# SwiGLU stages of a decoder trunk: the moving operands' addresses shifted against the standing operands'

## The chip, the cores and the metric

The kernel runs on one core of one Trainium2 chip. The metric is device time in microseconds (us) of one execution; lower is better. A core has a matrix engine (PE, with its weight loads listed apart as PEld), a vector engine (DVE), a scalar engine (ACT), GpSimd (POOL) and queues that start transfers (SP among them). It works on a scratch memory of 128 partitions; every address below is a byte address within a partition, the same in all 128.

## The reference

Two layers over x (512 tokens, width 1024, float32). In each, x takes half a SwiGLU, a mixer, and half a SwiGLU again, each after an RMSNorm:

```python
def _swiglu(h, wg, wu, wd):
    return (jax.nn.silu(h @ wg) * (h @ wu)) @ wd
...
    for l in range(DEPTH):
        h = _rmsnorm(x, ffn_pre_norm[l])
        x = x + 0.5 * _swiglu(h, ffn_pre_w_gate[l], ffn_pre_w_up[l], ffn_pre_w_down[l])
        ...
        h = _rmsnorm(x, ffn_post_norm[l])
        x = x + 0.5 * _swiglu(h, ffn_post_w_gate[l], ffn_post_w_up[l], ffn_post_w_down[l])
```

So there are four SwiGLU stages, with 2816 hidden columns each. The first layer's mixer is retention beside dilated attention, the second's is gated linear attention.

## The kernel before

All matrix products are done with operands split into a high and a low half (`hi` and `lo`, each 4 bytes an element), in three matmuls that add up in one accumulator: high by high, high by low, low by high. In a plain product (`mm3`, lines 205 to 207) the *standing* operand is a 128x128 piece of a weight tile (`whi`, `wlo`) and the *moving* one 512 tokens of an activation (`xgh`, `xgl`). Before each matmul PE loads the standing operand's 128 columns; that load shows as PEld.

In a SwiGLU stage (`ffn`) the first four hidden tiles go through plain products. The other 18 are made in pairs by the seven-product form (a Strassen-like scheme: seven products of half-size blocks in place of eight). `moving` builds its moving operands once for each stage: four tiles `hh` (high) and four `hl` (low), each seven slots of 256 tokens. `block_plan` loads a 1 MB piece of weights (`raw`) and makes the standing operands from it: `whi` and `wlo` for two of the seven products, and sums and differences of blocks, `shi` (made in `high`) and `slo` (made in `low`), for the other five. `product` then runs four k-steps of three matmuls, 256 moving columns each:

```python
    mm(out, lhsT=w[0][:, s], rhs=hi, ...)   # line 404: hh moving, whi or shi standing
    mm(out, lhsT=w[0][:, s], rhs=lo, ...)   # line 405: hl moving, the same standing
    mm(out, lhsT=w[1][:, s], rhs=hi, ...)   # line 406: hh moving, wlo or slo standing
```

Down products (`down_tile`, plain, 512 columns) are put between them. At the end of the last stage `last_half` runs plain products of 256 columns, half the tokens at a time.

Tiles of a stage come from one pool, `self.fpool`. A tile name gets its place when it is first asked for, right behind the one before. In a stage the order is `head`, `part` (2), `sg` (2), `hh` (4), `hl` (4), `raw` (2), `s3`, `space`, `shi` (6), `slo` (6). `space` is asked for in `high` at the first call of a stage, is never written, and only takes up room: 16 elements, 64 bytes. The long-lived tiles (`xgh`, `xgl`, `whi`, `wlo`) lie in other pools at fixed addresses.

**Distance**, in this text, is the address of a standing operand less that of the moving operand that streams while it is being loaded, as a remainder by 512 bytes. A standing piece is 512 bytes wide, a slot of `hh` 1024 and a row of 512 tokens 2048, so all pieces of a tile have the same remainder. In the program as built the remainders by 512 are:

```
tile                                  remainder     standing tile against it    distance
xgh, xgl (moving)                     384           whi, wlo 384                0
hh, hl (moving)                       320           whi, wlo, shi, slo 384      64
cath, catl of the first mixer         320           whi, wlo 384                64
cath, catl of the second mixer        0             whi, wlo 384                384
xgh (moving), ones_r (loaded)         384           ones_r 128                  256
diag (moving), whi (loaded)           96            whi 384                     288
xgh (moving), p (loaded)              384           p 320                       448
xgh (moving), sp (loaded)             384           sp 0                        128
```

`cath` and `catl` are the mixers' concatenated outputs, moving operands of their output projections (`out_steps`, 512 columns). `ones_r`, `p` and `sp` are small standing operands of the mixers and norms; each is loaded once or a few times right behind a plain product.

Of the kernel before, what the change touches and what calls it, by code (L numbers as in the profile page):

```python
# [19 lines left out]
P = 128  # L20
# [14 lines left out]
GROUPS = ((0, 1), (2, 3), (4, 5), (6, 7), (8,), (9, 10))  # L35
BLOCKS = ((2, 3), (4, 5), (6, 7), (8, 9), (10,))
XGB = 9

RET_HEADS, RET_DK = 4, 128
DIL_HEADS, DIL_DH = 8, 64  # L40
# [10 lines left out]
class Trunk:  # L51
    def __init__(self, ctx, tc, a):
# [3 lines left out]
        self.keep = pool("keep", bufs=1)  # L56
        self.xg = pool("xg", bufs=XGB)
        self.wpool = pool("wpool", bufs=4)
# [54 lines left out]
    def block_plan(self, src):  # L113


        nc = self.nc
        st = {}
        q = [slice(i * T, (i + 1) * T) for i in range(4)]

        def high(key, x):  # L120
            if not self.spaced:
                self.spaced = True
                self.t2k(self.fpool, "space", bufs=1, shape=[P, 16])
            hi = self.t2k(self.fpool, "shi", F32R, SUMS, shape=[P, T])
            nc.scalar.copy(out=hi, in_=x)  # L125
            st[key] = (hi, x)

        def low(key):
            hi, x = st[key]
            lo = self.t2k(self.fpool, "slo", F32R, SUMS, shape=[P, T])  # L130
            nc.vector.tensor_tensor(out=lo, in0=x, in1=hi.bitcast(F32), op=ALU.subtract)  # L131
            return hi, lo

        def add(out, a, b):
            nc.vector.tensor_tensor(out=out, in0=a, in1=b, op=ALU.add)  # L135

        def c0():
            raw = st["raw"] = self.t2k(self.fpool, "raw", shape=[P, 4 * T], bufs=2)
            nc.sync.dma_start(out=raw, in_=src)
            hi = self.t2k(self.wpool, "whi", F32R, shape=[P, WC])  # L140
            lo = self.t2k(self.wpool, "wlo", F32R, shape=[P, WC])
            nc.scalar.copy(out=hi, in_=raw[:, :WC])
            st["s3"] = self.t2k(self.fpool, "s3", bufs=1)
            add(st["s3"], raw[:, q[0]], raw[:, q[2]])
            add(raw[:, q[2]], raw[:, q[2]], raw[:, q[3]])
            high("s1", raw[:, q[2]])
            nc.vector.tensor_tensor(out=lo, in0=raw[:, :WC], in1=hi.bitcast(F32), op=ALU.subtract)
            add(raw[:, q[0]], raw[:, q[0]], raw[:, q[2]])
            return hi, lo

        def s1():
            high("s2", st["raw"][:, q[0]])
            return low("s1")

        def s2():
            raw = st["raw"]
            high("s3", st["s3"])
            add(raw[:, q[1]], raw[:, q[1]], raw[:, q[0]])
            return low("s2")

        def s3():
            high("a22", st["raw"][:, q[3]])
            return low("s3")

        def a22():
            high("s4", st["raw"][:, q[1]])
            return low("a22")

        def s4():
            return low("s4")  # L170

        return [("w", c0), ("s", s1), ("s", s2), ("s", s3), ("s", a22), ("s", s4)]
# [269 lines left out]
    def ffn(self, f, nxt):  # L442
        nc, tc = self.nc, self.tc
        gi = (0, 2, 3, 5)[f]
        with tc.tile_pool(name=self.uid("ffn"), bufs=1, reuse_waits="tile") as self.fpool, self.banks(pj=7, sc=1):
            self.act, self.hs, self.spaced = [], [], False
            new_sg = lambda: self.t2k(self.fpool, "sg", bufs=2, shape=[P, 2 * T])

            def glu(g, u, out):
                us = self.t2k(self.fpool, "part", bufs=2, shape=[P, 3 * H])[:, :T]  # L450
                nc.vector.tensor_tensor(out=out, in0=g, in1=self.rrow, op=ALU.mult)
                nc.scalar.activation(out=out, in_=out, func=AF.Silu)
                nc.vector.tensor_tensor(out=us, in0=u, in1=self.rrow, op=ALU.mult)
                nc.vector.tensor_tensor(out=out, in0=us, in1=out, op=ALU.mult)


            held, heads = [], []
            build = self.moving(gi)

            def head():  # L460
                n, g, u = held.pop(0)
                if n % 2 == 0:
                    heads.append(self.t2k(self.fpool, "head", shape=[P, 2 * T], bufs=1) if n == 0 else new_sg())
                glu(g, u, heads[-1][:, n % 2 * T:(n % 2 + 1) * T])

            for n in range(2 * HEAD):
                held.append((n, self.proj_t(), self.proj_t()))
                if n > 0:
                    head()
                    next(build, None)  # L470
                    next(build, None)
            head()
            for sg in heads:
                self.keep_act(sg)

            for before, group in zip(GROUPS, BLOCKS):
                calls = 4 * len(group)
                order = [KD * (i + 1) // calls - KD * i // calls for i in range(calls)]
                tiles = iter(range(KD))
                share = iter(order)  # L480

                def fill():
                    for _ in range(next(share)):
                        self.down_tile(next(tiles), before, False, nxt)

                for p in group:
                    sg = new_sg()
                    a, c = self.block(fill)
                    nc.scalar.activation(out=sg[:, :T], in_=c[:, :T], func=AF.Silu)
                    nc.scalar.activation(out=sg[:, T:T + H], in_=a[:, :H], func=AF.Silu, scale=-1.0)  # L490
                    nc.scalar.activation(out=sg[:, T + H:], in_=c[:, T:], func=AF.Silu, scale=-1.0)
                    a, c = self.block(fill)
                    neg = dict(scalar=-1.0, op0=ALU.mult, op1=ALU.mult)
                    nc.vector.tensor_tensor(out=sg[:, :T], in0=c[:, :T], in1=sg[:, :T], op=ALU.mult)
                    nc.vector.scalar_tensor_tensor(out=sg[:, T:T + H], in0=a[:, :H], in1=sg[:, T:T + H], **neg)
                    nc.vector.scalar_tensor_tensor(out=sg[:, T + H:], in0=c[:, T:], in1=sg[:, T + H:], **neg)
                    self.keep_act(sg)
            self.last_group(GROUPS[-1], nxt)
# [22 lines left out]
    def last_group(self, group, nxt):  # L521
# [5 lines left out]
        for d in range(KD):  # L527
# [14 lines left out]
            for e, w, at, ps in first:  # L542
# [4 lines left out]
                nc.vector.scalar_tensor_tensor(out=self.x[e], in0=ps, scalar=0.5, in1=self.x[e], op0=ALU.mult, op1=ALU.add)  # L547
                if nxt is not None and e < XGB - n:
                    self.scaled(e, nxt)
                self.squares(e)  # L550
            first = []
        if nxt is not None:
            for e in range(XGB - n, KD):
                self.scaled(e, nxt)
# [561 lines left out]
```

## Time and profile before

| what | value |
|---|---|
| median of 3 runs | 1919.24 us (1919.2 to 1923.63) |
| the profiled execution | 1920.47 us, span 1918.7 us |
| PE busy | 1889.4 us, 98% of the span |
| DVE, ACT busy | 1383.0 us (72%), 850.2 us (44%) |
| mean granted clock of TensorE | 0.993 of full speed |

Busy time of PE says little by itself: matmuls overlap in the profile (one of 256 columns is listed with 281 ns, and the next starts long before its end). What counts is the time from one matmul's start to the next one's start, called a **pass** below. Lines of the timeline give start and duration in us; L404 is line 404 of the kernel before, and an arrow reads output from inputs.

### The profile page before, as it was taken

Reading aid. Unit: us, or ns where it says so; the run is one execution under the profiler, and the core shown is the slowest. Engines: PE = TensorE matmul, PEld = TensorE weight load, DVE = VectorE, ACT = ScalarE, POOL = GpSimd, SP = SyncE. Lnnn points to the kernel's source line nnn. Section 1 sums busy time; section 2 is a strip of 40 time slices with the busy share of each in tenths; the row PEclk is TensorE's granted clock in tenths of the full one; section 3 lists DMA queues with packets and bytes.
Section 4 is the critical chain, followed back from the end, with each engine's and each line's share of the span. In section 5 each row is a group of like instructions: output and inputs, shape, how many; then the busy total and the mean of one; then the engine's idle time right before and its main releaser. Section 6 shows DMA issues by size and latency. Waiting matters only on the chain.

```text
span 1918.7 us, 28135 instructions
## 1 busy us (share of the span) xinstructions
PE 1889.4 (98%) x11360; PEld 1660.4 (87%) x11360; DVE 1383.0 (72%) x2114; ACT 850.2 (44%) x1377; POOL 90.1 (5%) x69
## 2 busy tenths in 40 slices
PE   8999999999999999999999999999999999999996
PEld 6899999877777889999988999998788888999995
DVE  7987786744555897777679878776466579777864
ACT  5544444433332554444445444444434245544441
POOL 1000000200000200000020000002000020000001
PEclk9999999999999999999999999999999999999998
DMA  5222222321111423332132322222222142323211
GB/s 199 99 104 106 100 100 78 123 77 66 50 66 39 165 88 112 109 104 105 67 124 92 110 103 100 99 89 85 88 77 67 56 156 89 118 100 110 100 67 44
DMA packets 43061, 183.81 MB, mean 96 GB/s; under 512 B 4897, under 2 KB 7201, under 8 KB 33714
## 3 DMA queue, kind: packets, MB, share of 16 engines
q1 hardware_dynamic: 39888, 177.75, 26.6%
q10 hardware_dynamic: 3042, 4.26, 0.7%
q8 instruction: 89, 1.46, 0.3%
q14 instruction: 42, 0.34, 0.1%
HBM read 179.89 MB, written 2.10 MB: 95 GB/s over the span
## 4 chain that ended last, share of the span: by engine, by line
PE 95%; DVE 3%; issue 1%; ACT 0%; POOL 0%; DMA 0%; POOLq 0%; DVEq 0%; SPq 0%; ACTq 0%
PE pj L205 17%; PE pj L206 17%; PE pj L207 17%; PE pj L404 12%; PE pj L406 12%; PE pj L405 12%; PE sc L740 1%; PE o L768 1%; PE sc L280 1%; PE sc L298 0%; PE sc L815 0%; PE tp L756 0%; DVE xgl L253 0%; DVE wlo L107 0%; PE o L972 0%
## 5 line engine op out<-in xcount | busy, mean ns | idle before, releaser
L205 PE MATMUL pj<-xgh,whi 128*128 128x512 f32 x1260 | 506.2, 402 | 8.0 <-ACT whi L106 7.1
L206 PE MATMUL pj<-xgl,whi 128*128 128x512 f32 x1260 | 493.2, 391 | 1.1 <-DVE xgl L253 1.0
L207 PE MATMUL pj<-xgh,wlo 128*128 128x512 f32 x1260 | 492.6, 391 | 0.0
L405 PE MATMUL pj<-hl,shi 128*128 128x256 f32 x1440 | 404.9, 281 | 1.5 <-DVE hl L394 1.5
L404 PE MATMUL pj<-hh,shi 128*128 128x256 f32 x1440 | 405.0, 281 | 0.8 <-ACT hh L392 0.8
L406 PE MATMUL pj<-hh,slo 128*128 128x256 f32 x1440 | 404.7, 281 | 0.0
L106 ACT CAST whi<-wraw 128x1024 fp32r<-128x1024 f32 x189 | 197.8, 1047 | 254.2 <-PE pj L206 164.1
L125 ACT CAST shi<-raw 128x512 fp32r<-128x512 f32 x288 | 178.5, 620 | 288.1 <-PE pj L405 232.6
L205 PEld LDWEIGHTS pj<-xgh,whi 128*128 128x128 f32 x1260 | 238.2, 189 | 62.0 <-issue 12.1
L107 DVE TENSOR_TENSOR wlo<-wraw,whi 128x1024 fp32r<-128x1024 f32 x189 | 236.1, 1250 | 65.5 <-ACT whi L106 64.9
L207 PEld LDWEIGHTS pj<-xgh,wlo 128*128 128x128 f32 x1260 | 237.9, 189 | 50.3 <-DVE wlo L107 0.8
L406 PEld LDWEIGHTS pj<-hh,slo 128*128 128x128 f32 x1440 | 276.6, 192 | 0.1
L206 PEld LDWEIGHTS pj<-xgl,whi 128*128 128x128 f32 x1260 | 238.2, 189 | 43.2 <-DVE xgl L253 2.2
L405 PEld LDWEIGHTS pj<-hl,shi 128*128 128x128 f32 x1440 | 270.5, 188 | 4.6 <-DVE hl L394 1.7
L404 PEld LDWEIGHTS pj<-hh,shi 128*128 128x128 f32 x1440 | 270.5, 188 | 4.0 <-ACT hh L392 1.1
L131 DVE TENSOR_TENSOR slo<-raw,shi 128x512 fp32r<-128x512 f32 x288 | 197.1, 687 | 83.4 <-ACT shi L125 83.3
L405 PE MATMUL pj<-hl,whi 128*128 128x256 f32 x576 | 162.3, 282 | 0.5 <-DVE hl L393 0.5
L404 PE MATMUL pj<-hh,whi 128*128 128x256 f32 x576 | 162.3, 282 | 0.1
L406 PE MATMUL pj<-hh,wlo 128*128 128x256 f32 x576 | 162.0, 281 | 0.0
L135 DVE TENSOR_TENSOR raw<-raw 128x512 f32<-128x512 f32 x216 | 148.5, 688 | 3.0
L519 DVE SCALAR_TENSOR_TENSOR x<-pj,x 128x512 f32<-128x512 f32 x160 | 109.6, 685 | 50.7 <-PE pj L207 50.7
L270 POOL TENSOR_TENSOR sqa<-sqa,sq 128x512 f32<-128x512 f32 x41 | 64.0, 1561 | 1061.8 <-issue 645.2
(201 smaller groups left out, 2375.0 us busy)
## 6 DMA issues: line engine op xcount, KB each, us to landing
raw<-in_w_blk SPq DMA_DIRECT2D x72, 1024.0 KB, 4.8
wraw<-in_w_down SPq DMA_DIRECT2D x88, 512.0 KB, 3.2
wraw<-in_w_gu SPq DMA_DIRECT2D x32, 512.0 KB, 3.2
wraw<-in_w_dqk SPq DMA_DIRECT2D x8, 512.0 KB, 3.4
wraw<-in_w_rqk SPq DMA_DIRECT2D x8, 512.0 KB, 3.3
wraw<-in_w_eo SPq DMA_DIRECT2D x8, 512.0 KB, 3.2
wraw<-in_w_gr SPq DMA_DIRECT2D x8, 512.0 KB, 3.3
wraw<-in_w_gv SPq DMA_DIRECT2D x8, 512.0 KB, 3.2
```

The costliest lines, as they stand in the source:

```text
L106: self.halved = nc.scalar.copy(out=hi[:, :cols], in_=raw[:, :cols]).ins
L107: nc.vector.tensor_tensor(out=lo[:, :cols], in0=raw[:, :cols], in1=hi[:, :cols].bitcast(F32), op=ALU.subtract)
L125: nc.scalar.copy(out=hi, in_=x)
L131: nc.vector.tensor_tensor(out=lo, in0=x, in1=hi.bitcast(F32), op=ALU.subtract)
L135: nc.vector.tensor_tensor(out=out, in0=a, in1=b, op=ALU.add)
L205: mm(out, lhsT=w[0], rhs=x[0], start=first, stop=False)
L206: mm(out, lhsT=w[0], rhs=x[1], start=False, stop=False)
L207: self.last = mm(out, lhsT=w[1], rhs=x[0], start=False, stop=last).ins
L404: mm(out, lhsT=w[0][:, s], rhs=hi, start=first and k == 0, stop=False, skip_group_check=True)
L405: mm(out, lhsT=w[0][:, s], rhs=lo, start=False, stop=False, skip_group_check=True)
L406: self.last = mm(out, lhsT=w[1][:, s], rhs=hi, start=False, stop=k == KD // 2 - 1, skip_group_check=True).ins
L519: nc.vector.scalar_tensor_tensor(out=self.x[d], in0=ps, scalar=0.5, in1=self.x[d], op0=ALU.mult, op1=ALU.add)
```

## The change

Each stage gets a number of its own from `SHIFTS`. A tile `shift` of that many elements, never written, is asked for first in the stage's pool, so all tiles up to `s3` lie that much higher. `space` grows to 144 elements less the shift, so `shi` and `slo` lie 512 bytes higher in all four stages and keep their remainder.

```diff
+SHIFTS = (32, 48, 64, 80)
...
         def high(key, x):
             if not self.spaced:
                 self.spaced = True
-                self.t2k(self.fpool, "space", bufs=1, shape=[P, 16])
+                self.t2k(self.fpool, "space", bufs=1, shape=[P, 144 - self.shift])
...
             self.act, self.hs, self.spaced = [], [], False
+            self.shift = SHIFTS[f]
+            self.t2k(self.fpool, "shift", bufs=1, shape=[P, self.shift])
```

From the two programs as built, the remainders of `hh` and `hl` and their distance to the standing operands:

```
stage (f)   shift, bytes   hh, hl before   hh, hl after   distance before   distance after   after, by 256
1 (0)       128            320             448            64                448              192
2 (1)       192            320             0              64                384              128
3 (2)       256            320             64             64                320              64
4 (3)       320            320             128            64                256              0
```

No instruction is added, removed or moved: on all five engines the two programs list the same instructions in the same order. The waits are the same too, but for two transfers at the head of stage 3 (line 139, `raw`): the first `raw` now waits for two earlier transfers where it waited for one, and the second for none where it waited for one, because the shifted buffer overlaps both `raw` buffers of stage 2.

## Rows read from the trace of the kernel before

**Rows 1.** The page, busy time by engine and the chain that ended last.

```profile
PE 1889.4 (98%) x11360; PEld 1660.4 (87%) x11360; DVE 1383.0 (72%) x2114; ACT 850.2 (44%) x1377; POOL 90.1 (5%) x69
...
PE 95%; DVE 3%; issue 1%; ACT 0%; POOL 0%; DMA 0%; POOLq 0%; DVEq 0%; SPq 0%; ACTq 0%
```

**Rows 2.** Windows of stages 1 and 4, line 404 alone: window, length, PE busy, PEld.

```profile
55.28:336.50 281.22, 142.32 (x504) 94.80 (x503) 0.99 0.28 100
...
1600.51:1873.79 273.28, 141.62 (x504) 94.42 (x503) 1.00 0.28 99
```

**Rows 3.** Timeline, seven-product form: start us, duration us, engine, line.

```profile
318.34 0.28 PE L404 MATMUL pj<-hh,shi 128*128 128x256 f32 x1
318.34 0.19 PEld L405 LDWEIGHTS pj<-hl,shi 128*128 128x128 f32 x1
...
320.46 0.28 PE L404 MATMUL pj<-hh,shi 128*128 128x256 f32 x1
```

**Rows 4.** Timeline, plain products of 256 columns at the end of stage 4.

```profile
1895.67 0.28 PE L206 MATMUL pj<-xgl,whi 128*128 128x256 f32 x1
...
1897.47 0.28 PE L206 MATMUL pj<-xgl,whi 128*128 128x256 f32 x1
```

**Rows 5.** Timeline, plain products of 512 columns, xgh and xgl moving.

```profile
1888.07 0.39 PE L205 MATMUL pj<-xgh,whi 128*128 128x512 f32 x1
...
1891.47 0.39 PE L205 MATMUL pj<-xgh,whi 128*128 128x512 f32 x1
```

**Rows 6.** Timeline, first mixer's output projection, cath and catl moving.

```profile
609.83 0.39 PE L206 MATMUL pj<-catl,whi 128*128 128x512 f32 x1
...
612.16 0.39 PE L207 MATMUL pj<-cath,wlo 128*128 128x512 f32 x1
```

**Rows 7.** Timeline, second mixer's output projection, cath and catl moving.

```profile
1529.71 0.40 PE L207 MATMUL pj<-cath,wlo 128*128 128x512 f32 x1
...
1532.04 0.40 PE L207 MATMUL sc<-cath,wlo 128*128 128x512 f32 x1
```

**Rows 8.** Timeline, a plain product followed by a matmul on ones_r.

```profile
1346.25 0.39 PE L207 MATMUL pj<-xgh,wlo 128*128 128x512 f32 x1
1346.25 0.19 PEld L298 LDWEIGHTS sc<-diag,ones_r 128*128 128x128 f32 x1
...
1346.47 0.40 PE L298 MATMUL sc<-diag,ones_r 128*128 128x512 f32 x1
1346.71 0.40 PE L205 MATMUL pj<-xgh,whi 128*128 128x512 f32 x1
```

**Rows 9.** Timeline, a plain product followed by transposes of p.

```profile
444.94 0.40 PE L207 MATMUL pj<-xgh,wlo 128*128 128x512 f32 x1
444.95 0.48 PEld L756 LDWEIGHTS tp<-ident,p 128*128 128x128 f32 x3
...
445.18 0.38 PE L756 MATMUL tp<-ident,p 128*128 128x128 f32 x2
```

**Rows 10.** Timeline, a plain product followed by matmuls on sp.

```profile
1453.94 0.40 PE L207 MATMUL pj<-xgh,wlo 128*128 128x512 f32 x1
1453.95 0.54 PEld L965 LDWEIGHTS o<-e,sp 128*128 128x128 f32 x3
...
1454.18 0.38 PE L965 MATMUL o<-e,sp 128*128 128x128 f32 x2
```

**Rows 11.** Timeline, short matmuls of the second mixer, 128 moving columns each.

```profile
1442.16 1.06 PE L939 MATMUL sc<-e,e 128*128 128x128 f32 x8
1443.05 1.06 PE L877 MATMUL sc<-cum,la 128*128 128x128 f32 x8
```

**Rows 12.** Head of stage 3: last reads of raw, its first transfer, first use.

```profile
L131 DVE TENSOR_TENSOR slo<-raw,shi x3: 685/693/693, 939.4 to 947.9; 128x512 fp32r<-128x512 f32 x3
...
959.64 0.42 SPq L139 DMA_DIRECT2D raw<-in_w_blk  x1
...
972.78 0.68 DVE L135 TENSOR_TENSOR s<-raw 128x512 f32<-128x512 f32 x1
```

## The prediction

> **What bounds the kernel now.** I read the page first. PE is busy 98% of the span, and the chain that ended last lies on PE for 95% [rows 1]; no other engine is near. So the time changes if a matmul's pass changes, and hardly otherwise. Then the windows by stage: line 404 has 504 matmuls in each stage [rows 2], lines 405 and 406 as many, so the seven-product form has 3 x 504 = 1512 passes a stage and 6048 in all. The granted clock there is 0.99 to 1.00 [rows 2] of full speed, the level of 2.4 GHz. Then the timeline, for the pass itself. From 318.34 to 320.46 there are 18 passes in 2.12 us, 117.8 ns each [rows 3]. 6048 such passes are 712 us, 37% of the span. That is the part of the time that the change can touch.
>
> The reader should also see in [rows 3] when the next standing operand is read: the load for line 405 starts at 318.34, with the matmul of line 404. So PE reads two streams at a time, the moving one of this matmul and the standing one of the next, and the address between them is what the change alters.
>
> **Does the address matter?** The trace has other distances. With 512 columns, xgh and xgl moving against whi and wlo (distance 0) take 15 passes in 3.40 us, 226.7 ns [rows 5]. The output projections do the same work with cath and catl moving: 10 passes in 2.33 us, 233 ns, at distance 64 [rows 6], and again 2.33 us for 10 at distance 384 [rows 7]. With 256 columns, the end of stage 4 has distance 0: 15 passes in 1.80 us, 120.0 ns [rows 4], against 117.8 at distance 64 in the seven-product form [rows 3]. So it matters by 2 to 6 ns, and not in the same direction: 0 is the cheaper of the two at 512 columns and the dearer at 256. With 256 columns the moving stream is so short that the load lies beside all of it; either stream can be the one that is late.
>
> A rule of the Trainium skill speaks against any effect. "TensorE: Matmul & The Clock Gate", section "Step-by-step: what each phase is for", gives PE two independent read ports and says that loading the next weights takes no bandwidth from the running matmul; "SBUF — State Buffer", section "Who interferes with whom", says that PE never waits on anyone. By that rule the sum below is 0 in every stage; the trace disagrees, with 117.8 against 120.0 ns and 226.7 against 233 ns for equal work at different addresses.
>
> **After what distance does the pattern repeat?** Single passes of 512 columns help. While ones_r is loaded the distance is 256: that pass goes from 1346.25 to 1346.47, 0.22 us, and the next, diag against whi at distance 288, takes 0.24 [rows 8]. There are eleven passes like the first (32.79 to 1566.98 us); ten last 226 to 228 ns, as at distance 0, and one 230. At distance 448 (p) the pass is 0.24 us [rows 9] and at 128 (sp) also 0.24 [rows 10]; the others on p and sp right behind xgh take 230 to 238 ns. So at 512 columns 256 acts like 0, and 128, 448, 64, 384 and 288 all act unlike it. I take it that the pattern repeats every 256 bytes. Starts are rounded to 10 ns in these rows and each is a single pass, so this is likely, not sure.
>
> **The change, part by part.** The two tiles that only take up room cost no instruction, and every engine's list is the same as before, so nothing queues differently. One wait is new: the first raw transfer of stage 3 has to find both raw buffers of stage 2 free. The last read of raw in stage 2 starts at 947.9 and takes 0.7 us, the transfer starts at 959.64, and its data is first used at 972.78 [rows 12]. It finds both free for 11 us, so this costs 0; were that cover gone, a transfer would have the 13 us to its first use before PE noticed. The plain products keep their addresses and cost 0. What is left is 1512 passes a stage, each at its new distance:
>
> Stage 3, distance 320, which is 64 by 256: the pass of now, 117.8 ns, and 0 us. If the pattern does not repeat by 256, it is as open as stages 1 and 2.
>
> Stage 4, distance 256, which is 0 by 256: the nearest rows of the same width are [rows 4], 120.0 ns. 1512 x 2.2 ns = +3.4 us.
>
> Stage 1 (448, or 192 by 256) and stage 2 (384, or 128): no pass of 256 columns at these distances is in the trace. From below: a pass can't be shorter than its load. Eight matmuls of 128 columns, which hide none of it, take 0.89 us from 1442.16 to 1443.05, 111.2 ns each [rows 11]; 117.8 less 111.2 is 6.5 ns, so at best -9.9 us a stage. From above: the largest steady difference between two distances is the 6.3 ns from [rows 5] to [rows 6], so +9.5 us a stage; the largest seen at 256 columns is 2.2 ns, +3.4 us. At 512 columns 448, 384 and 128 belong with 64, not with 0 [rows 6, 7, 9, 10], so I put both stages at the row of 64, 117.8 ns, and 0 us.
>
> The sum is 0 + 0 + 0 + 3.4 = +3.4 us. On the profiled execution, 1920.47 us (1.8 us more than its span), that makes 1923.9. The profiled execution was 1.2 us above the median of the runs, 1919.24, so the median should be 1922.6 us, 0.18% up. A measurement of this kernel can tell about 0.3% from no change, 5.8 us, which is 0.95 ns on each of the 6048 passes.
>
> **The rivals.**
>
> *64 is the one good distance at 256 columns, and the others cost what 0 costs.* For it: the only other distance seen at this width is the dearer one, and at 512 columns too there is one good class and a wide bad one. Against it: at 512 columns 128, 384 and 448 go with 64. It is decided by stages 1 and 2. If one of them takes 120.0 ns, the sum is +6.7 us, 1926.0; if both do, +10.1 us, 1929.3; with stage 3 too, +13.4 us, 1932.7. From two of the four stages on it is slower by over 0.3%.
>
> *At 128 or 192 the two streams keep clear of each other and the load alone sets the pass.* This is the other side: faster. For it: 117.8 is still 6.5 ns above what a load takes alone [rows 3, 11], so some conflict is left at distance 64, and a place half a period away may avoid it. Against it: at 512 columns no distance gets below the 226.7 ns of distance 0, and the two streams, one covering 1024 bytes while the other covers 512, must cross at some point wherever they start. One stage at 111.2 ns makes -9.9 + 3.4 = -6.5 us, 1912.7; both make -16.4 us, 1902.9. It comes out faster by over 0.3% once stages 1 and 2 together give back 9.2 us, that is 3 ns a pass.
>
> *The change does nothing:* the 2.2 ns between [rows 3] and [rows 4] come from the code around them (last_half is a short run behind a stage, with other tiles), not from the distance. Then 1919.2. Against it: the 15 passes of [rows 4] are all alike, and [rows 5] and [rows 6] do equal work. The rule of the Trainium skill named above ("TensorE: Matmul & The Clock Gate") ends here too.
>
> **How the numbers follow.** My forecast (stage 4 dearer, the rest within a few tenths of a ns) gets 0.46. No effect gets 0.08, and mixtures in which a loss and a gain nearly cancel 0.04. The first rival, in one of its forms, gets 0.29, and the second 0.13. So within 0.3%: 0.46 + 0.08 + 0.04 = 0.58; slower 0.29; faster 0.13. The range reaches down to one stage at the load's floor, 1912.7, rounded to 1912, and up to both stages 1 and 2 at 120.0 ns, 1929.3, rounded to 1930. It leaves out about 0.07 below (both stages at the floor) and 0.11 above (stage 3 too, or passes over 120 ns).
>
> **What the profile after would show.** Stage by stage, count the passes in a stretch like [rows 3]: I expect 117.8 ns in stages 1, 2 and 3 and 120.0 in stage 4, and stage 4's window longer by 3.4 us with the others unchanged. Stage 3 away from 117.8 says that the pattern doesn't repeat by 256. Stage 4 at 117.8 says that [rows 4] were about something else. Stage 1 or 2 at 111 is the second rival, and at 120 or above the first. The plain products should stay at 226.7 ns, and PE should not wait for raw at the head of stage 3. The prediction is wrong if the four stages' mean pass moves by more than 0.95 ns; the least supported step is that 128 and 192 do what 64 does.

## The result and the profile after

The changed kernel takes 1930.72 us in the median (1928.43 to 1933.4, 4 runs) beside 1919.22 us (1918.98 to 1923.63, 4 runs) for the kernel before on the same chip. The ratio is 1.0055, with a 95% interval of 1.0034 to 1.0076: 0.55% slower, by more than the 0.3% named above. The forecast was 1922.6 us and no change that can be told; the median is 0.7 us above the top of the range.

From the page of the changed kernel, busy time by engine and the chain that ended last, to be put beside [rows 1]:

```profile
PE 1902.5 (98%) x11360; PEld 1668.7 (86%) x11360; DVE 1383.9 (72%) x2114; ACT 851.1 (44%) x1377; POOL 90.1 (5%) x69
...
PE 95%; DVE 3%; issue 1%; ACT 0%; POOL 0%; DMA 0%; POOLq 0%; DVEq 0%; SPq 0%; ACTq 0%
```

As many instructions as before on every engine, and the chain still lies on PE: what moved is the time of PE's own passes. The windows of the four stages, line 405 alone (the line that was 404), set from a stage's first seven-product matmul to its last, to be put beside [rows 2] (window, length, PE busy, PEld busy, granted clock, DMA share, GB/s):

```profile
54.93:337.25 282.32, 141.77 (x504) 94.75 (x503) 0.99 0.29 100
691.39:969.32 277.93, 141.55 (x504) 95.42 (x503) 1.00 0.29 102
1042.29:1315.48 273.19, 141.59 (x504) 94.42 (x503) 1.00 0.29 101
1609.36:1886.60 277.24, 142.40 (x504) 96.43 (x503) 1.00 0.28 98
```

Before, the same stretches (start of the first to start of the last seven-product matmul) were 281.09, 273.16, 273.16 and 273.16 us in the trace. So the third stage is exactly as long as before, the first is 1.2 us longer, the second 4.75 and the fourth 4.05. Now the passes, as in [rows 3], from the timeline of the changed kernel (start us, duration us, engine, line). The pairs stand 18 passes apart, in stages 1, 2, 3 and 4; the last pair is the first and the twelfth plain product behind a seven-product stretch of stage 2, 11 passes apart:

```profile
234.58 0.28 PE L407 MATMUL pj<-hh,slo 128*128 128x256 f32 x1
...
236.70 0.28 PE L407 MATMUL pj<-hh,wlo 128*128 128x256 f32 x1
...
834.19 0.28 PE L407 MATMUL pj<-hh,slo 128*128 128x256 f32 x1
...
836.35 0.28 PE L407 MATMUL pj<-hh,wlo 128*128 128x256 f32 x1
...
1182.66 0.28 PE L407 MATMUL pj<-hh,slo 128*128 128x256 f32 x1
...
1184.78 0.28 PE L407 MATMUL pj<-hh,wlo 128*128 128x256 f32 x1
...
1751.81 0.28 PE L407 MATMUL pj<-hh,slo 128*128 128x256 f32 x1
...
1753.97 0.28 PE L407 MATMUL pj<-hh,wlo 128*128 128x256 f32 x1
...
839.00 0.39 PE L206 MATMUL pj<-xgh,whi 128*128 128x512 f32 x1
...
841.53 0.39 PE L208 MATMUL pj<-xgh,wlo 128*128 128x512 f32 x1
```

Stages 1 and 3 take 2.12 us for 18 passes, 117.8 ns each; stages 2 and 4 take 2.16 us, 120.0 ns. And the eleven plain passes take 2.53 us, 230 ns each, where [rows 5] have 226.7. In the trace's nanoseconds those passes are 233, 233, 236, 224, 231, 236, 228, 232, 231, 227, 227: they settle, and they end at the pass of before. The same twelve plain products in the kernel before run at 226 and 227 from the first one on. The ledger of the stages, worked out from the starts in both traces (plain settling is the sum of the plain passes inside the stage less 226.67 ns each; the last column is the difference of the stretches above):

```
stage   distance   mean pass ns   passes us   plain settling us   stage longer by us
1       448        117.87         +0.1        +1.25               +1.2
2       384        119.90         +3.2        +1.54               +4.75
3       320        117.78          0           0                   0
4       256        119.81         +3.1        +0.98               +4.05
sum                               +6.4        +3.8                +10.0
```

In the first stage waits at its head gave back 0.2 us; that head varies by as much from run to run. The gap between stages 2 and 3 moved by 0.05 us (72.94 to 72.99), so the wait for both `raw` buffers is hidden, as [rows 12] said; after, the transfer starts at 965.19 and is first used 13.3 us later (timeline, queue and DVE):

```profile
965.19 0.38 SPq L140 DMA_DIRECT2D raw<-in_w_blk  x1
...
978.45 0.68 DVE L136 TENSOR_TENSOR s<-raw 128x512 f32<-128x512 f32 x1
```

The spans of the two profiled executions differ by 12.9 us, not by 10.0. Ahead of the first stage's seven-product passes 0.3 us were given back, and 3.2 us were added in the second mixer, where the granted clock fell in this execution and not in the profiled one of before. From the windows of the changed kernel, the last figures but two being the granted clock:

```profile
1350.00:1360.00 10.00, 10.00 (x41) 7.23 (x40) 4.67 (x7) 4.06 (x6) 0.00 (x0) 1.00 0.31 105
1361.00:1367.00 6.00, 6.00 (x13) 3.63 (x12) 0.00 (x0) 4.61 (x5) 0.00 (x0) 0.50 0.27 87
1370.00:1380.00 10.00, 10.00 (x46) 8.28 (x45) 4.94 (x6) 2.11 (x2) 0.00 (x0) 1.00 0.18 59
```

Kernels with the distances of before show the same drop in some of their executions (the run at distance 320 below was profiled in one, 1923.14 us, while its fastest was 1918.06), so it is not the change's. The two executions of the changed kernel at a mean clock of 0.994 took 1928.43 and 1929.17 us, 9.4 to 10.2 us above the fastest of before, 1918.98, which is about the ledger's +10.0.

### The profile page after: what moved, and what is told of

Read it like the earlier page. It is cut to its first block, busy times and chain, and to the rows that moved or that the text cites. A ratio compares the mean times of both kernels' runs of the same rounds, so it can differ in the third digit from the quotient of the medians.

```text
span 1931.6 us, 28136 instructions
## 1 busy us (share of the span) xinstructions
PE 1902.5 (98%) x11360; PEld 1668.7 (86%) x11360; DVE 1383.9 (72%) x2114; ACT 851.1 (44%) x1377; POOL 90.1 (5%) x69
## 4 chain that ended last, share of the span: by engine, by line
PE 95%; DVE 3%; issue 1%; ACT 0%; POOL 0%; DMA 0%; POOLq 0%; DVEq 0%; SPq 0%; ACTq 0%
PE pj L206 17%; PE pj L207 17%; PE pj L208 17%; PE pj L407 12%; PE pj L405 12%; PE pj L406 12%; PE sc L743 1%; PE o L771 1%; PE sc L281 1%; PE sc L299 0%; PE sc L818 0%; PE tp L759 0%; DVE xgl L254 0%; DVE wlo L108 0%; PE o L975 0%
```

## The experiments

Up to the run at 480, the kernels are the changed kernel with other numbers for its four stages, unless the heading says otherwise; from there on they are the kernel before with the edit shown. All distances in what follows are by 256.

**All four stages at distance 320, 64 by 256.**

```diff
-SHIFTS = (32, 48, 64, 80)
+SHIFTS = (64, 64, 64, 64)
```

> All four stages get the shift of 64 elements, so the distance is 320 in each (64 by 256); hh, hl, raw and the rest lie 256 bytes higher and shi, slo 512 bytes higher than in the kernel before. If the distance by 256 is what counts: 117.8 ns a pass in all four stages, the plain products among them at 226.7 ns with no settling, and 1919 us, within 0.3% of before. If the cost comes from moving the tiles at all (other absolute addresses, raw overlapping two buffers, shi 512 bytes higher): three or four stages as dear as stages 2 and 4 of the changed kernel, about 4 us each, 1931 to 1935 us.

1918.79 us in the median of 10, ratio 0.9999 (0.9989 to 1.001). The later three stages are steady at 117.78 ns and 273.16 us long, with plain products at 226.67 ns; the first has the same passes but for part of one stretch, to which the open questions below come back. Timeline of its first stage, 18 passes apart:

```profile
233.92 0.28 PE L407 MATMUL pj<-hh,slo 128*128 128x256 f32 x1
...
236.04 0.28 PE L407 MATMUL pj<-hh,wlo 128*128 128x256 f32 x1
```

To read: all tiles of the stage moved, one more transfer waited, and nothing was lost. So the cost of the change comes with the distance, not with the move.

**Distances 0 and 256 in turn.**

```diff
-SHIFTS = (32, 48, 64, 80)
+SHIFTS = (16, 80, 16, 80)
```

> Shifts of 16, 80, 16 and 80 elements: distance 0 in stages 1 and 3, 256 in stages 2 and 4. If the pattern repeats every 256 bytes: all four stages alike, 119.8 to 120 ns a pass (the 119.8 of stage 4 in the changed kernel), each about 4 us longer, 4 x 4.05 = 16 us, 1935 us. If the pattern repeats only by 512: stages 1 and 3 differ from 2 and 4 by more than 0.3 ns a pass. If absolute addresses count: no rule ties the stages together, and stages 2 and 4 need not be alike.

1935.16 us (4 runs), ratio 1.0079 (1.006 to 1.0097). The passes average 119.80, 119.81, 119.83 and 119.82 ns, the later three stages are 277.21 us long (+4.05 each), and the plain products settle for 0.95 to 0.99 us a stage. Timeline of stage 3, distance 0:

```profile
1187.56 0.28 PE L407 MATMUL pj<-hh,slo 128*128 128x256 f32 x1
...
1189.72 0.28 PE L407 MATMUL pj<-hh,wlo 128*128 128x256 f32 x1
```

2.16 us for 18, as in stage 4 of the changed kernel: 0 and 256 are the same distance for this machine, and [rows 4], 15 passes at the end of the kernel, had the right price for a whole stage.

**Only the weight sums moved by 64 bytes (the kernel before, `space` 32 wide).** `shi` and `slo` stand at 128, `whi` and `wlo` stay at 64.

```diff
-                self.t2k(self.fpool, "space", bufs=1, shape=[P, 16])
+                self.t2k(self.fpool, "space", bufs=1, shape=[P, 32])
```

> The kernel before with the room ahead of shi at 32 elements in place of 16: hh and hl stay where they were, shi and slo lie 64 bytes higher. Distance 64 against whi and wlo as before, 128 against shi and slo (4248 of the 6048 passes). If the distance between the two streams of a pass counts: passes that load shi or slo at about 119.9 ns, those that load whi or wlo at about 117.8; 4248 x 2.1 ns = 9 us, and up to 1.5 us a stage of settling in the plain products, 1928 to 1934 us. If the moving tiles' own address counts: nothing moved that streams, all passes 117.8 and 1919 us.

1923.09 us (10 runs), ratio 1.0014 (1.0005 to 1.0024): far less than expected. Passes that load at 128 averaged 118.42 ns instead of 119.9, those that load at 64 only 115.9 instead of 117.8; the mean of all is 117.68, a little *less* than before. Two products at different distances do not cost what each of them costs alone: in all 54 long stretches of the later three stages the twelve passes at 64 behind a product at 128 come down to 113 and 114 ns, which no stage with one distance showed. The stages are longer by 0.80 us all the same, and the plain products' settling alone is 0.95 us. So this run has the settling without dearer seven-product passes: it is a cost of its own. Timeline behind a stretch of stage 2, two steps of 5 plain passes:

```profile
836.88 0.39 PE L205 MATMUL pj<-xgh,whi 128*128 128x512 f32 x1
...
838.03 0.39 PE L207 MATMUL pj<-xgh,wlo 128*128 128x512 f32 x1
...
839.17 0.39 PE L206 MATMUL pj<-xgl,whi 128*128 128x512 f32 x1
```

The first five take 1.15 us, 230 ns each, the next five 1.14; in the trace's nanoseconds 232, 233, 230, 227, 227 and then 226, 227, 227, 226, 227.

**Steps of 32 bytes, and the period once more.** The first run has distances 32, 224, 160, 96, the second 128, 192, 224, 96 at other addresses.

```diff
-SHIFTS = (32, 48, 64, 80)
+SHIFTS = (8, 24, 40, 56)
```

> Shifts of 8, 24, 40 and 56 elements: distances 32, 480, 416 and 352, which are 32, 224, 160 and 96 by 256, the places between those seen so far. If only the 64-byte block counts that an address lies in: 32 like 0 or 64, 96 like 64 or 128, and so on, each stage at 117.8 or 119.8 to 120 ns. If there is a better place than 64, one of the stages shows a pass under 117.7 ns. If conflicts grow when the two addresses are not a multiple of 64 apart, all four are over 120 ns.

```diff
-SHIFTS = (32, 48, 64, 80)
+SHIFTS = (112, 96, 24, 120)
```

> Shifts of 112, 96, 24 and 120 elements: distances 128, 192, 480 and 96. Three of them are 256 bytes from distances already measured: 384 (119.9 ns a pass), 448 (117.87) and 352 (118.78). If the pattern repeats every 256 bytes and only the distance counts, stage 1 takes 119.9, stage 2 117.87, stage 4 118.78 ns, and stage 3 the 116.73 of 480, in another stage than before. If the pattern repeats by 512 only, stages 1, 2 and 4 differ from these by more than 0.3 ns. The kernel in which shi alone moved had 118.4 ns on the passes at distance 128; if stage 1 takes 119.9 here, those 118.4 came from the passes before them, not from a period of 512.

1929.58 and 1928.3 us, one execution each. Timeline of the second one in stages 1 and 3 (128 and 224), 18 passes apart:

```profile
236.44 0.28 PE L407 MATMUL pj<-hh,slo 128*128 128x256 f32 x1
...
238.60 0.28 PE L407 MATMUL pj<-hh,wlo 128*128 128x256 f32 x1
...
1182.10 0.28 PE L407 MATMUL pj<-hh,slo 128*128 128x256 f32 x1
...
1184.20 0.28 PE L407 MATMUL pj<-hh,wlo 128*128 128x256 f32 x1
```

With the runs so far this gives a price for each distance in steps of 32, where all seven products of a stage have the same one and the plain products between them stay at 0 (mean of all passes of a stage, and settling of the stage's plain products):

```
distance by 256          0      32     64     96     128    160    192    224
mean pass ns             119.8  118.3  117.8  118.8  119.9  120.1  117.9  116.7
plain settling us        1.0    1.3    0      0.3    1.5    1.5    1.3    0.8
```

Distances 0, 64, 96, 128 and 192 were each met at both remainders by 512 (as 128 and 384), and the two agree to 0.05 ns: the pattern repeats every 256 bytes. It is not one good place and a bad rest, and the distance with the shortest pass, 224, is not that of before.

**All stages at 480, 224 by 256.**

```diff
-SHIFTS = (32, 48, 64, 80)
+SHIFTS = (24, 24, 24, 24)
```

> Shift of 24 elements in all four stages, distance 480 (224 by 256), the one place whose pass was under 117.78 ns. If passes add up as measured in one stage (1512 x -1.05 = -1.6 us, and +0.84 us of settling in the plain products, -0.74 us a stage): -3.0 us, 0.16% faster than before, 1916 us. If the settling of the plain products costs more in the other stages, no change. The changed kernel's lesson read backwards: the gain is smaller than the 6.4 us that the passes alone promise.

1917.85 us (11 runs), ratio 0.9991 (0.9982 to 1.0). The passes average 116.73 ns and the later three stages are 272.42 us long, 0.74 less than before: 1511 passes at 1.05 ns less are 1.6 us, of which the settling takes 0.84 back. In the medians that is hardly to be told from no change. But the four executions at a mean clock of 0.994 took 1914.82 to 1915.24 us, beside 1917.55 to 1918.27 for the four of the kernel before at that clock, and the difference of their means is the 3.0 us that was expected.

**Plain products at other distances (the kernel before, 64 bytes of room behind each `whi` and `wlo` tile).** Now the four tiles stand at distances 0, 64, 128 and 192 from `xgh` and `xgl`; weight sums stay at 64.

```diff
-        return self.cut(self.wpool, "w", raw, cols, WC)
+        return self.cut(self.wpool, "w", raw, cols, WC + 16)
...
-            hi = self.t2k(self.wpool, "whi", F32R, shape=[P, WC])
-            lo = self.t2k(self.wpool, "wlo", F32R, shape=[P, WC])
+            hi = self.t2k(self.wpool, "whi", F32R, shape=[P, WC + 16])[:, :WC]
+            lo = self.t2k(self.wpool, "wlo", F32R, shape=[P, WC + 16])[:, :WC]
```

> The kernel before with 64 bytes of room behind each of the four whi and wlo tiles: plain products at distances 0, 64, 128 and 192 by 256, one weight tile after the other, with the same code and the same xgh and xgl. If the distance makes the 233 ns of the output projections, plain products on the three shifted tiles settle at about 233 ns and those on the unshifted at 226.7; if it is the output projections' own tiles and waits, all stay at 226.7. Stretches of 24 passes have one distance each, so the first nine or so of a stretch may still be settling. In total some 3000 plain passes x 6 ns = 18 us or less, 1925 to 1945 us.

1916.1 us in one execution. Past the 12th pass of a stretch, plain passes average 226.8 ns at distance 0, 233.3 at 64, 232.7 at 128 and 228.8 at 192: the 233 ns of [rows 6] are the distance, not the output projection. But the kernel did not get slower. Timeline of stage 2: eleven plain passes at distance 64, then two stretches of 18 seven-product passes, both with 64 by 256 throughout:

```profile
832.82 0.39 PE L206 MATMUL pj<-xgh,whi 128*128 128x512 f32 x1
...
835.38 0.39 PE L208 MATMUL pj<-xgh,wlo 128*128 128x512 f32 x1
...
811.36 0.28 PE L406 MATMUL pj<-hl,whi 128*128 128x256 f32 x1
...
813.40 0.28 PE L406 MATMUL pj<-hl,shi 128*128 128x256 f32 x1
...
836.08 0.28 PE L406 MATMUL pj<-hl,shi 128*128 128x256 f32 x1
...
838.20 0.28 PE L406 MATMUL pj<-hl,shi 128*128 128x256 f32 x1
```

The eleven plain passes take 2.56 us, 233 ns each. The 18 passes take 2.04 us in the first stretch, 113.4 ns, and 2.12 us in the second, 117.8. In the trace's nanoseconds the one goes 113, 113, 114 and on, the other 118, 117, 119, 117, 118, 118. Both are steady for as long as the stretch lasts, at one distance. Below, 117.8 ns at distance 64 is called the dear state and 113.3 ns the cheap state. All seven-product passes of the run average 115.19 ns, and the later three stages are 270.27, 270.27 and 272.56 us long.

**The same with 32 bytes of room, for all weight tiles, and 128 more between two of them.** Plain products at 32 and 96 by 256 in the first three stages, at 0 and 64 in the last.

```diff
-        return self.cut(self.wpool, "w", raw, cols, WC)
+        return self.cut(self.wpool, "w", raw, cols, WC + 8)
...
+        if not self.padded:
+            self.padded = True
+            self.t2k(self.wpool, "wmid", bufs=1, shape=[P, 32])
...
```

> As the run with 64-byte steps, but 32 bytes of room behind each whi and wlo tile and 128 bytes between the two groups: plain products at 0, 32, 64 and 96 by 256 (whi) and the same by 256 for wlo. If plain products have a better place than 0, as the seven-product form had at 224, it shows as a stretch under 226 ns; if 0 is their best place, no stretch does. The distances of the seven-product form change too in this run, so only the plain stretches are read.

1923.46 us in one execution. Plain passes past the 12th take 233.3 ns at 32, 234.0 at 96, 233.4 at 64 and 226.8 at 0, so no place beat 0; seven-product passes average 115.73 ns, again with both steady states at distance 64. After this run the question was no longer which distance is best, but what puts a stretch at 64 into the state of 113.3 ns. In these two runs a product at 32, 128 or 224 ahead of it always did (54 times), one at 192 did 104 times in 107, one at 0 never (72 times), and neither did plain products at 0. Theory one, in the next three runs, is that the order of distances before a pass chooses its state; in the last run it becomes that the address that jumps counts too.

**Opening products at 192, by the moving tiles.** Slots 0 and 6 of `hh` and `hl`, which open the two stretches of a block pair, go to 192: the tile lies 128 bytes higher, a gap of 128 bytes brings the other slots back to 64, and `space` grows so that the weight sums keep their place by 256. The tile is built in more and smaller copies (cut here).

```diff
-                self.t2k(self.fpool, "space", bufs=1, shape=[P, 16])
+                self.t2k(self.fpool, "space", bufs=1, shape=[P, 48])
...
-        ts = slice(slot * H, (slot + 1) * H)
+        ts = slot * H + 32 * ((slot > 0) + (slot == 6))
+        ts = slice(ts, ts + H)
...
+            self.t2k(self.fpool, "shift", bufs=1, shape=[P, 32])
```

> In two earlier runs the 256-column passes at one and the same distance of 64 ran steadily either at 117.78 ns (118, 117, 119) or at 113.33 ns (113, 113, 114). Which of the two seems to be set by the passes just before: out of a plain stretch at distance 0 it was always the dear one, out of a product at distance 192 it was the cheap one after four passes (115, 116, 123, 118). Here plain products stay at distance 0, and the two products that open a stretch of seven-product passes (slots 0 and 6 of the moving tiles) go to distance 192, all others stay at 64. Theory one (two steady states, the passes before choose): the opening 12 passes cost 117.8 ns, the 48 behind them in the longer stretch 113.3 but for four, the 12 in the shorter one likewise; per stage pair of stretches 44 x 4.45 + 8 x 4.45 - 4 = 228 ns less, times 72 = 16.4 us; each of 144 entries into plain products settles for about 15 ns (as after the cheap state before: 232, 232, 231, 227), 2 us back; the time is about 1905 us, ratio 0.9926. Rival (the cheap state comes only where the plain products before run at 231 to 236 ns): all passes stay at 117.8 ns, 1919 to 1921 us. More: the moving tiles are built with eight more small copies and subtractions per pair, in the head of the stage, expected to be hidden.

1922.05 us (11 runs), ratio 1.001 (1.0001 to 1.0019); all passes average 117.76 ns. The passes are the rival's, so theory one failed as it stood. One long stretch, in stage 4, fell to 113.3 ns all the same, twelve passes behind the step to 64 and right behind two passes of 122 and 125 ns. Of the 2.7 us above before, 1.3 are in the profiled first stage, where the tiles are built; the rest was not followed up.

**Opening product at 192, by the standing tile.** The first weight tile of a block lies 128 bytes into a wider tile.

```diff
-        return self.cut(self.wpool, "w", raw, cols, WC)
+        return self.cut(self.wpool, "w", raw, cols, WC + 64)
...
-            hi = self.t2k(self.wpool, "whi", F32R, shape=[P, WC])
-            lo = self.t2k(self.wpool, "wlo", F32R, shape=[P, WC])
+            hi = self.t2k(self.wpool, "whi", F32R, shape=[P, WC + 64])[:, 32:32 + WC]
+            lo = self.t2k(self.wpool, "wlo", F32R, shape=[P, WC + 64])[:, 32:32 + WC]
```

> Only the first weight tile of each block (used by its first and its fourth product) is put at distance 192, through its own place inside a wider tile; everything else stays at 64, plain products at 0. Theory one (two steady states, the passes before choose): first product 117.8 ns, then four settling passes, then 113.3 ns through the other 44 passes, those at 192 in the fourth product too; 44 x 4.45 - 2 = 194 ns in each of 72 longer stretches, 14.0 us less; the shorter stretches stay at 117.8; 72 exits into plain products at 15 ns give 1.1 us back: about 1906 us, ratio 0.993. Rival (distance alone counts, or the plain products before must be dear): 192 costs 117.9 and 64 costs 117.8, so 1919 to 1921 us.

1916.72 us (11 runs), ratio 0.9988 (0.9979 to 0.9997). Half of theory one's way: the step from 192 to 64 behind the first product led to the dear state, that behind the fourth product, from the same two distances, to the cheap one. Timeline of a stretch in stage 2, the third product and the fifth, 11 passes each:

```profile
830.49 0.28 PE L404 MATMUL pj<-hh,shi 128*128 128x256 f32 x1
...
831.79 0.28 PE L406 MATMUL pj<-hh,slo 128*128 128x256 f32 x1
...
833.32 0.28 PE L404 MATMUL pj<-hh,shi 128*128 128x256 f32 x1
...
834.57 0.28 PE L406 MATMUL pj<-hh,slo 128*128 128x256 f32 x1
```

1.30 us against 1.25, 118 and 113.4 ns in the trace's nanoseconds, at the same distance, and so in all 54 long stretches of the later three stages. The two came by different ways: the first product at 192 followed plain products, the second followed products at 64.

**That way, made by the moving tiles: slot 3, which the second product uses, at 192.** The way is plain 0, then 12 passes at 64, 12 at 192, 36 at 64.

```diff
...
-        ts = slice(slot * H, (slot + 1) * H)
+        ts = slot * H + 32 * ((slot > 2) + (slot > 3))
+        ts = slice(ts, ts + H)
```

> The cheap state of distance 64 (113.3 ns instead of 117.78) was entered in all 72 long stretches of the run before behind one order of products: plain at 0, a product at 64 in the dear state, twelve passes at 192 (122, 118, 117, 119, ...), then 64 (116, 114, 114, 113, 113, 114). It was not entered from plain at 0 straight to 192 and then 64 (119, 117, 118, 117). Here only slot 3 of the moving tiles, which the second product of the longer stretch uses, goes to distance 192; first weight tile, plain products and the other slots stay as before. Theory one (the order of distances before a pass chooses the state, and the same order chooses the same one): the first 24 passes 117.8 ns, the 36 behind them 113.3 but for two, so 36 x 4.45 - 5 = 155 ns less in each of 72 longer stretches, 11.2 us, of which about 1.1 us is given back as the plain products behind settle: 1909 us, ratio 0.9947; mean of all seven-product passes 115.9. Rival (only the longer history, 36 passes ahead of the switch instead of 12, did it): the passes stay at 117.8 and the time at 1919 to 1920 us.

1920.82 us (11 runs), ratio 1.0009 (1.0 to 1.0018), all passes of the later three stages at 117.78 ns: no cheap state in any of their stretches. Into 192 the passes read 119, 118, 120, 117, as they had in the run on slots 0 and 6.

**The same way, made by the standing tile: only the weight sum of the second product at 192.** The helper gives the tile of that sum 128 bytes more (the tiles' own remainders alternate, so the offset does too).

```diff
+        def half_row(tag, key):
+            odd = {"shi": (0, 1, 0, 1, 0, 1), "slo": (0, 1, 0, 1, 1, 0)}[tag][self.turn[tag] % SUMS]
+            self.turn[tag] += 1
+            at = 32 if odd != (key == "s1") else 0
+            return self.t2k(self.fpool, tag, F32R, SUMS, shape=[P, T + 32])[:, at:at + T]
...
-            hi = self.t2k(self.fpool, "shi", F32R, SUMS, shape=[P, T])
+            hi = half_row("shi", key)
...
-            lo = self.t2k(self.fpool, "slo", F32R, SUMS, shape=[P, T])
+            lo = half_row("slo", key)
...
```

> The same order of distances as in the run with slot 3 at 192 (plain 0, twelve passes at 64, twelve at 192, then 64), but made by the standing tile: only the weight sum of the second product is moved by 128 bytes within a wider tile, and every moving address stays where it was before. In the two runs behind, 64 to 192 by the moving address read 119, 118, 120, 117 and led back to 117.8 ns; by the standing address (first weight tile at 192) it read 122, 118, 117, 119 and led to 113.3. Theory one (not the distance alone: a jump of the standing address against the load before it, and a jump of the moving address against the matmul before it, leave different phases): the 36 passes behind run at 113.3, the mean of all seven-product passes is 115.9, the time about 1909 us, ratio 0.995. Rival (the longer history ahead of the switch did it): all at 117.8 ns, the switch reads 119, 118, 120, and the time stays at 1919 to 1921 us.

1909.03 us (1908.44 to 1911.66, 5 runs), ratio 0.9948 (0.9935 to 0.9962), with 1909 expected. Page line, the window of stage 2, and the timeline of one long stretch there (products one, two, three and four, 11 passes each):

```profile
PE 1878.5 (98%) x11360; PEld 1648.7 (86%) x11360; DVE 1381.9 (72%) x2114; ACT 850.5 (45%) x1377; POOL 90.1 (5%) x69
```

```profile
687.35:957.90 270.55, 140.44 (x504) 94.42 (x503) 1.00 0.30 105
```

```profile
824.04 0.28 PE L410 MATMUL pj<-hh,whi 128*128 128x256 f32 x1
...
825.34 0.28 PE L412 MATMUL pj<-hh,wlo 128*128 128x256 f32 x1
825.45 0.28 PE L410 MATMUL pj<-hh,shi 128*128 128x256 f32 x1
...
826.75 0.28 PE L412 MATMUL pj<-hh,slo 128*128 128x256 f32 x1
826.87 0.28 PE L410 MATMUL pj<-hh,shi 128*128 128x256 f32 x1
...
828.11 0.28 PE L412 MATMUL pj<-hh,slo 128*128 128x256 f32 x1
828.23 0.28 PE L410 MATMUL pj<-hh,whi 128*128 128x256 f32 x1
...
829.47 0.28 PE L412 MATMUL pj<-hh,wlo 128*128 128x256 f32 x1
```

1.30, 1.30, 1.24 and 1.24 us: products one and two at 118 ns, three and four (and five) at 113. The mean of all passes in a later stage is 115.85 ns, the stage is 270.52 us long instead of 273.16, and the plain products give 0.27 us back. The same instructions on every engine as in the kernel before, at other addresses, are 0.5% faster than it; this is the fastest kernel of the study. Its order of distances is that of the run on slot 3. What differs is which of the two addresses jumps by 128 bytes between products, and with it one pass: the next weights are loaded while the product before still streams, so the lengths are 11, 12 and 37 passes here and 12, 12 and 36 there. Into 192 the passes read 118, 117, 119, without the 122 of the run on the first weight tile.

## Why the prediction was off

By the sign that the prediction set for itself it was wrong: the mean pass of the four stages moved by 1.06 ns (the mean of the ledger's four, 118.84, less 117.78), more than 0.95.

**Right.** PE's passes are the whole of it: instructions, chain and the other engines stood still. Where all seven products of a stage stand at one distance, the distance sets the pass, and the rival that the change does nothing fell with the run at 0 and 256. The pattern repeats every 256 bytes, so stage 3 kept its 117.8 ns and its length. Stage 4 took 119.81 ns against 120.0 forecast, +3.1 us against +3.4. Stage 1 took 117.87 against 117.8. The new wait for `raw` cost nothing.

**Wrong, first: "At 512 columns 448, 384 and 128 belong with 64, ... so I put both stages at the row of 64".** This was the step that the prediction called its least supported. It held for 192 (stage 1) and not for 128 (stage 2), which took 119.90 ns, +3.2 us. This was the rival in which one more stage costs what 0 costs, 1926.0 us; its bound, the 2.2 ns seen at 256 columns, was the right one. The classes of one width say nothing of the other: at 512 columns the good distance is 0 (226.8 ns) and 64 the bad one (233.3), at 256 columns it is nearly the reverse. Nor was 192 in the class where I had put it: at 512 columns it takes 228.8 in steady stretches, where [rows 9] were single passes.

**Wrong, second: "The plain products keep their addresses and cost 0".** They keep their addresses and still take 3.8 us more. Behind each stretch at 128, 192 or 0 they need 5 to 9 passes to come back to 226.7 ns; behind a stretch at 64 in its dear state they need none. The run with only the weight sums moved shows this term alone: 0.95 us a stage, with the seven-product passes no dearer. [Rows 3] and [rows 5] are steady stretches and could not show it; what the trace did show, and the prediction passed over, is that every plain stretch inside a stage is only 12 passes long. With both terms the sum is 0.1 + 3.2 + 0 + 3.1 + 3.8 = +10.2 us, 1929.4 us on the median of before, against 1928.43 and 1929.17 us where the clock held.

That the top of the range, +10.1 us for stages 1 and 2 both at 120.0 ns, comes so near is luck: stage 1 stayed at 117.87 ns, and in place of its 3.4 us stand 3.8 us of settling, for which the range had no term.

**The rival on the other side** fell here: no stage came near the load's 111.2 ns [rows 11]. That this is what a load takes by itself was taken from those eight matmuls, and no run tests it. But the room under 117.8 that spoke for the rival is there: the cheap state runs at 113.3 ns.

**A wrong idea under the whole working** was that a distance has a pass. The kernel before had only one entry into its seven-product stretches, plain products at 0, and so showed only one of the two states of distance 64.

**Open.** Why there are two states, and what exactly picks one. Shown is that the order of distances does not settle it: the run on slot 3 and the run on one weight sum have the same order but for one pass, and end at 117.8 and 113.3 ns. A jump of the standing address led to the cheap state in one step of two (first weight tile at 192), in the last run, and behind 128 in the run with only the weight sums moved; a jump of the moving address alone did not in two runs. But no jump is needed. In the run at 320, where every product stands at 64, one long stretch of the first stage changed its state behind one late pass (timeline of that run, distance 64 throughout, granted clock 1.00):

```profile
94.33 0.28 PE L405 MATMUL pj<-hh,whi 128*128 128x256 f32 x1
...
96.45 0.35 PE L405 MATMUL pj<-hh,shi 128*128 128x256 f32 x1
96.64 0.28 PE L406 MATMUL pj<-hl,shi 128*128 128x256 f32 x1
...
96.99 0.28 PE L406 MATMUL pj<-hl,shi 128*128 128x256 f32 x1
...
99.03 0.28 PE L406 MATMUL pj<-hl,whi 128*128 128x256 f32 x1
```

The 18 passes up to 96.45 take 2.12 us, 117.8 ns each; the next one takes 187 ns; the 18 from 96.99 take 2.04 us, 113.3 ns each, and the rest of the stretch stays there. At the same place of the stretch a pass of 180 ns led from dear to cheap in the run on the first weight tile, one of 197 ns from cheap to dear in the run with 64 bytes of room, and one of 192 ns left the kernel before in the dear state. So the state hangs on the timing of single passes too, and not on addresses alone. That this is a phase between the two streams, carried from pass to pass, fits all runs, the settling too, but no run measures the phase or says which delay picks which state. Nor does one separate which address jumps from the one pass by which the jump comes earlier. I also did not try to bring the shorter stretches into the cheap state.

## What to carry to other kernels

In this kernel, where PE streams short matmuls back to back with loads of 4-byte weights, the addresses of the two operands by 256 bytes are worth about 3% of a pass (116.7 to 120.1 ns at 256 columns, 226.8 to 234.0 at 512), and at one distance the cheap state is 3.8% under the dear one. In another kernel, read it from the start-to-start time of a long run, for each width by itself. Don't price a form from its own steady rows alone: what ran before it can leave a short stretch in another state, and what runs behind it pays for settling. When an address experiment comes out better than its parts, look at the single passes: the gain of 0.5% here was found in a run that was made to show a loss.

## What was not expected of the hardware

At one distance, one width and a granted clock of 1.00, 256-column passes are steady at 117.78 ns (pattern 118, 117, 119, 117, 118, 118, 118, 117, 118, nine passes long) or at 113.33 (113, 113, 114), and one late pass of 187 ns moved a stretch from the first to the second. At 128 and 160 the steady passes swing: 118, 120, 122 and 121, 117, 125, 115, 124, 118. Plain passes of 512 columns need up to nine passes, 2.1 us, to forget what ran before.

The page "TensorE: Matmul & The Clock Gate" of the Trainium skill, in "Step-by-step: what each phase is for", has two independent read ports, and loading as free beside a running matmul. The runs disagree by up to 6.8 ns a pass: 120.1 against 113.3 ns for the same instructions at other addresses.

The granted clock fell to 0.50, the level of 1.2 GHz, for some 7 us around 1364 us in the profiled execution of the changed kernel and, as long or shorter, in those of most other runs, but not in those of the kernel before and of the run at 480. Before it fell, PE had gone from 512-column products to products over 17 rows (line 868 of the changed kernel); the kernel before has the same order of products. The fall cost 3.2 us here, as much as one stage's term.
